# Side stages of a hybrid encoder layer, placed anew among its matmuls: later delta inverses, gates by themselves, scores two tiles ahead, x loaded earlier

## The chip, the cores and the metric

The kernel runs on one core of one Trainium2 chip. The metric is the device time of one execution in microseconds (us); where several runs are given, their median counts. The engines are named as the profile names them: PE is TensorE, DVE is VectorE, ACT is ScalarE, POOL is GpSimd, and SP is SyncE, whose instruction stream issues the DMAs.

## The reference, cut to what matters

One layer of an encoder works on 2048 prompt rows (zero state) and on 64 sample rows of a running stream (past of 2048 rows). A projection feeds four mixers with four heads of 64 each; their outputs are normed, gated and projected, and an MLP follows:

```python
proj = jnp.matmul(x, w_in)                       # 1024 -> 3856 columns, split among the mixers
o_a, gdn_s_new = _gated_delta(qa, ka, va, beta, g, gdn_s)     # A: chunks, triangular solve, state
o_b = _stick_breaking(qb, k_all, v_all, past)                 # B: attention with a running sum over keys
h_c, ... = _mlstm(qc, kc, vc, i_pre, log_f, c, n, m)          # C
o_d, ... = _hgrn2(silu(q), k_d, v, log_f, s)                  # D
mix = jnp.matmul(o, w_out);  x = layernorm(ALPHA * x + mix)
x = layernorm(ALPHA * x + jnp.square(relu(x @ w1 + b1)) @ w2 + b2)
```

In A each chunk needs the inverse of a unit lower triangular matrix (`triangular_solve(eye + lm, rhs)`), and a state that goes from chunk to chunk. In B the weight of a key is `exp(log_sigmoid(z) + after)`, where `after` sums over all later keys, so the key tiles of a query block depend on each other through a carry.

## The kernel before

The 2048 rows are 16 token tiles of 128, in four blocks of four tiles; block 0 also takes the sample's 64 rows. Two tiles make a unit, and the sample is a unit of its own: nine units. Every product with a large matrix is done with three matmuls on a split of both factors into a rounded part and a remainder (`mm3`, L463 to L466: `whi`/`wlo` of the weights, `XH`/`XL` of x, which `split_T`, L478 to L480, makes with transposes). A weight tile is read once into a ring `raw` (L455), split by ACT (L456) and POOL (L457), written to DRAM and read back from there whenever it is used again.

The program's stages are generators. `dense()` runs the projection of the four blocks and then the MLP of the four blocks, with the mixing of outputs (`mix`) in between; it is the main one. The others are `places()` (x into place, transposed), `delta()` (per unit: `gates`, then `gdn`), `memories()` (`mlstm`, `hgrn`) and `attend()`. `interleave` (L404) puts their pieces into one order by a clock of its own: a piece yields (PE time, delay until the next piece is due). The main stage goes first whenever it is due; the others get a turn when the main stage can't go, or when `EVERY` = 2.5 us of that clock have passed. `flag` and `need` order the stages among each other. Only PE keeps exactly this order. The order of DVE, ACT, POOL and SP is made by the framework's scheduler, which takes what its own estimate says is ready first; every engine then runs its list strictly in order.

Pieces of these stages that matter here:

- `gdn` (L870 on): per unit the conv, the products of keys and queries (L927, L928), transposes (L936, L937), then a solve of 16x16 blocks on DVE in 15 steps (L959 to L965) whose results go through DRAM (`ud`, `wd`) into the tiles `W` and `WT`. Two rounds of doubling follow for a unit of 128-row chunks: L994 multiplies the masked `cu` (POOL, L988) with `WT`, L1001 the result with `W`, L1009 transposes back; L1017 and L1024 do the last doubling. Then each chunk runs the recurrence (L1038 to L1059). The delay before the first L994 is 30 us of the planner's clock.
- `gates` (L762 to L838): small tiles, transposes, and row vectors through DRAM. It stands in `delta()` ahead of `gdn` of the same unit; its PSUM tiles come from the delta rule's ring (tag `m`, one bank) and its rows from the ring `g1`.
- `attention` (L1323 on), for each head: for each key tile `scores` (L1352, L1353), `stick` (the bound on DVE, L1317 or L1320; exp and ln on ACT, L1282 and L1283), `add_carry` (a row added on DVE, L1292; a cast on ACT, L1294; a remainder on POOL, L1295), `sums` (L1302, L1303: PE sums over later keys with a triangular matrix), `weights` (DVE L1309, ACT L1310 and L1312, DVE L1313) and `add_up` (L1362, L1363). Scores of the next key tile are issued right behind the `sums` of this one.
- `into_place` (L568): a tile of x is loaded in two halves from the ring `x2` (L486), one tile ahead of its transposes. `x2` also holds what leaves the projection.

## Time and profile before

| what | us |
|---|---|
| time, median of 3 runs | 3519.49 (3518.52 to 3526.22) |
| the profiled execution: its own time | 3528.34 |
| the profiled execution: its span | 3526.4 |
| PE busy in it | 3181.5 (90%) |
| DVE, ACT and POOL busy | 2239.1, 1345.4, 841.9 |
| mean granted clock of PE | 0.946 |

The span is that of the instructions in the trace; the execution's own time has about 2 us around it. PE's busy time counts a matmul from start to end although matmuls overlap, so it isn't PE at its peak. A row of PE's groups gives, behind the last bar, how long PE sat idle just before such an instruction, and what ended that.

### The profile page before, as it was taken

What the parts mean: (1) busy time and instruction counts of PE and PEld (TensorE: products, weight loads), DVE (VectorE), ACT (ScalarE), POOL (GpSimd) and SP (SyncE); (2) the same over time, 40 slices, a digit from 0 to 9 for tenths busy, and PEclk for the clock granted to TensorE, in tenths of its full rate; (3) what the DMA queues carried; (4) which work ended last, traced back from release to release, by engine and by line L of the source; (5) the groups of instructions that cost most, each with busy time, mean ns of one, the idle gap of its engine ahead of it and who ended that gap; (6) DMA issues with size and microseconds to landing.
All of it is one profiled execution on the core that took longest, in us unless ns stands there. A gap on an engine that the chain in (4) does not pass through costs nothing.

```text
span 3526.4 us, 60129 instructions
## 1 busy us (share of the span) xinstructions
PE 3181.5 (90%) x20906; PEld 2704.2 (77%) x20906; DVE 2239.1 (63%) x5360; ACT 1345.4 (38%) x3048; POOL 841.9 (24%) x946
## 2 busy tenths in 40 slices
PE   6897899898986988898898699999799999999998
PEld 6897888887875876676777488778577888888997
DVE  1566546344576777869688877787777554564445
ACT  2343433322343454654555454454454311121111
POOL 3342112101133134444435311221322100010001
PEclk8999998999998998999999799899899999999999
DMA  6986675566675875586678555567657587865552
GB/s 220 296 284 188 179 243 173 175 212 187 214 243 171 267 239 186 177 263 220 201 235 280 171 173 187 155 226 213 192 174 249 189 262 236 273 214 166 161 164 87
DMA packets 576268, 735.63 MB, mean 209 GB/s; under 512 B 104745, under 2 KB 301021, under 8 KB 575965
## 3 DMA queue, kind: packets, MB, share of 16 engines
q1 hardware_dynamic: 575964, 731.79, 64.9%
q8 instruction: 166, 2.72, 0.3%
q14 instruction: 138, 1.12, 0.1%
HBM read 548.63 MB, written 182.94 MB: 207 GB/s over the span
## 4 chain that ended last, share of the span: by engine, by line
PE 59%; DVE 17%; DMA 11%; SPq 4%; issue 4%; ACT 3%; POOL 2%; POOLq 0%; DVEq 0%; ACTq 0%
PE d L464 16%; PE d L465 16%; PE d L466 16%; DMA wlo<-wsp 1%; SPq L195 1%; DVE acc L1639 1%; DMA g<-qkv 1%; DMA vv<-x 1%; PE d L527 1%; PE a L1303 1%; DMA x<-in_x_prompt_dram 1%; DVE acc L1564 1%; DVE g L959 1%; POOL ar L1295 1%; DVE g L884 1%
## 5 line engine op out<-in xcount | busy, mean ns | idle before, releaser
L464 PE MATMUL d<-XH,whi 128*128 128x512 f32 (+1 forms) x1840 | 675.6, 367 | 3.7 <-ACT whi L456 3.0
L465 PE MATMUL d<-XL,whi 128*128 128x512 f32 (+1 forms) x1840 | 661.0, 359 | 1.0 <-DVE XL L480 0.9
L466 PE MATMUL d<-XH,wlo 128*128 128x512 f32 (+1 forms) x1840 | 659.8, 359 | 0.5 <-POOL wlo L457 0.5
L1639 DVE TENSOR_TENSOR acc<-d,acc 128x512 f32<-128x512 f32 x564 | 386.1, 687 | 177.6 <-PE d L466 164.7
L1295 POOL TENSOR_TENSOR ar<-as,ar 128x512 fp32r<-128x512 f32 (+3 forms) x177 | 198.2, 1120 | 956.5 <-ACT ar L1294 840.0
L464 PE MATMUL d<-whi,hh 128*128 128x512 f32 x992 | 404.9, 408 | 12.6 <-ACT x L1618 4.2
L465 PE MATMUL d<-wlo,hh 128*128 128x512 f32 x992 | 396.2, 399 | 0.1
L466 PE MATMUL d<-whi,hh 128*128 128x512 f32 x992 | 396.0, 399 | 0.0
L464 PEld LDWEIGHTS d<-XH,whi 128*128 128x128 f32 x1840 | 352.4, 192 | 53.7 <-ACT whi L456 3.2
L466 PEld LDWEIGHTS d<-XH,wlo 128*128 128x128 f32 x1840 | 351.7, 191 | 52.3 <-POOL wlo L457 0.9
L465 PEld LDWEIGHTS d<-XL,whi 128*128 128x128 f32 x1840 | 352.2, 191 | 46.6 <-DVE XL L480 1.4
L457 POOL TENSOR_TENSOR wlo<-raw,whi 128x512 fp32r<-128x512 f32 (+1 forms) x204 | 272.7, 1349 | 319.5 <-ACT whi L456 235.9
L464 PE MATMUL d<-whi,XH 128*128 128x256 f32 (+1 forms) x1024 | 316.3, 309 | 26.3 <-DMA whi<-wsp 15.4
L465 PE MATMUL d<-wlo,XH 128*128 128x256 f32 (+1 forms) x1024 | 307.9, 301 | 11.9 <-DMA wlo<-wsp 8.1
L466 PE MATMUL d<-whi,XL 128*128 128x256 f32 (+1 forms) x1024 | 305.3, 298 | 2.6 <-DVE XL L480 2.6
L1618 ACT ACTIVATE x<-d,cbig 128x512 f32<-128x512 f32 (+1 forms) x160 | 97.7, 610 | 506.4 <-PE d L466 502.6
L464 PEld LDWEIGHTS d<-whi,XH 128*128 128x128 f32 x1024 | 211.6, 207 | 32.5 <-DMA whi<-wsp 17.4
L464 PEld LDWEIGHTS d<-whi,hh 128*128 128x128 f32 x992 | 190.0, 192 | 57.2 <-ACT x L1618 5.1
L1620 DVE CAST hh<-x 128x512 fp32r<-128x512 f32 (+1 forms) x160 | 79.3, 496 | 236.2 <-ACT x L1619 235.8
L465 PEld LDWEIGHTS d<-wlo,XH 128*128 128x128 f32 x1024 | 211.3, 206 | 17.1 <-DMA wlo<-wsp 11.5
L466 PEld LDWEIGHTS d<-whi,hh 128*128 128x128 f32 x992 | 189.5, 191 | 44.4
L465 PEld LDWEIGHTS d<-wlo,hh 128*128 128x128 f32 x992 | 190.0, 192 | 41.2 <-DMA wlo<-wsp 0.8
(437 smaller groups left out, 6334.0 us busy)
## 6 DMA issues: line engine op xcount, KB each, us to landing
whi<-wsp SPq DMA_DIRECT2D x644, 256.0 KB
wlo<-wsp SPq DMA_DIRECT2D x644, 256.0 KB
wsp<-whi SPq DMA_DIRECT2D x196, 256.0 KB
wsp<-wlo SPq DMA_DIRECT2D x196, 256.0 KB
raw<-in_w_dram SPq DMA_DIRECT2D x128, 256.0 KB
raw<-in_w_in_dram SPq DMA_DIRECT2D x52, 256.0 KB
ak<-kk SPq DMA_DIRECT2D x80, 128.0 KB
ak<-vv SPq DMA_DIRECT2D x80, 128.0 KB
```

The source lines that it names most:

```text
L195: SP.dma_start(dst if dst.dtype == F32 else dst.bitcast(F32), src if src.dtype == F32 else src.bitcast(F32))
L457: POOL.tensor_tensor(lo, raw, hi.bitcast(F32), ALU.subtract)
L464: PE.matmul(out, lhsT=lh, rhs=rh, start=start, stop=False)
L465: PE.matmul(out, lhsT=lh, rhs=rl, start=False, stop=False)
L466: PE.matmul(out, lhsT=ll, rhs=rh, start=False, stop=stop)
L527: PE.matmul(pt, lhsT=lhs(k), rhs=r, start=k == ks[0] and i == 0, stop=k == ks[-1] and i == 1)
L884: DVE.scalar_tensor_tensor(dst[:, i], xin[:, i, j : j + N], convw(2 * p + i, j), dst[:, i], ALU.mult, ALU.add)
L959: DVE.tensor_tensor(tb[:PB, :m, :m], wb[:PB, i + 1 :, i + 1 :].rearrange("p j c -> p c j"), ub[:PB, i, i + 1 :].unsqueeze(1).to_broadcast( ...
L1295: POOL.tensor_tensor(sl, sp, sh.bitcast(F32), ALU.subtract)
L1618: ACT.activation(r, pt, AF.Relu, bias=b1c(ff))
L1620: DVE.tensor_copy(h[:, f, cs], r)
L1639: lambda pt, first, acc=acc: DVE.tensor_tensor(acc, pt, acc, ALU.add),
```

## The change

- The delays in `gdn` are raised: 30 to 50 before the first L994, 2.5 to 3.0, 2.0 to 3.5, 3.5 to 4.0, 3.0 to 4.0 and 1.5 to 2.5 at later places.
- `gates` becomes a stage of its own, `rows_of()`, that may run up to two units ahead. Its PSUM tiles move to the bank of `memories` (tag `h`), its rows to a ring `rw` of three.
- `interleave` gets a second list: `places` and `attend` are looked at whenever the planner comes round; `rows_of`, `delta` and `memories` still get a turn every 2.5 us. A channel-major step yields twice as often.
- `attention` issues the scores and `stick` of two key tiles at the start, and then those of tile x+2 behind the sums of tile x; the carry for tile x+1 is added directly behind the weights of tile x. Its delay goes from 7 to 6.5.
- `into_place` loads all tiles of a block at once, whole rows into the ring `acc`; `start` loads x1 at a flag `soon`, ahead of the free place.
- Rings: `raw` 4 to 3, `as` 4 to 5, `ak` 4 to 6.

```diff
-W_RAW, W_SP = 4, 6
+W_RAW, W_SP = 3, 6
-R_AS, R_AR, R_AQ, R_AK, R_OB = 4, 4, 3, 4, 1
+R_AS, R_AR, R_AQ, R_AK, R_OB = 5, 4, 3, 6, 1
+    rw = ring("rw", UNIT, 3)
...
-    def interleave(main, others):
+    def interleave(main, alike, others):
...
-            if not moved or clock[0] - last >= EVERY:
-                for g in sorted([g for g in alive if g is not main and due[id(g)] <= clock[0]], key=lambda g: due[id(g)]):
-                    moved = step(g) or moved
-                    last = clock[0]
+            turn = not moved or clock[0] - last >= EVERY
+            for g in sorted([g for g in alive if g in alike or turn and g in others], key=lambda g: due[id(g)]):
+                if due[id(g)] <= clock[0] and step(g):
+                    moved = True
+                    if g in others:
+                        last = clock[0]
...
-                if k % 4 == 3 and k < KD - 1:
-                    yield 12 * n * MM, 0
+                if k % 2 == 1 and k < KD - 1:
+                    yield 6 * n * MM, 0
...
     def into_place(b):
-        nxt = load_T(b.tiles[0], b.tiles[0].x)
+        ld = []
+        for t in b.tiles:
+            ld.append(bp.tile([P, 4 * UNIT], F32, tag="acc", name=nm("acc"), bufs=R_ACC)[:, :D])
+            SP.dma_start(ld[-1][: t.n], t.x)
+        if not b.i:
+            yield 0, 4
         for j, t in enumerate(b.tiles):
-            xt = nxt
             if b.i:
                 yield from need("xfree", b.i, j)
-            yield from put_T(t, t.off, xt)
-            if j + 1 < len(b.tiles):
-                nxt = load_T(b.tiles[j + 1], b.tiles[j + 1].x)
+            yield from put_T(t, t.off, [ld[j][:, 512 * g : 512 * g + 512] for g in range(2)])
...
-        pc = ps([C, 2 * w])
+        pc = ph([C, 2 * w])
...
-        ra, rb, rc = g1([68, N]), g1([68, N]), g1([68, N])
+        ra, rb, rc = rw([68, N]), rw([68, N]), rw([68, N])
...
-            yield (0.9, 30) if bs == 16 else (0.8, 2.5)
+            yield (0.9, 50) if bs == 16 else (0.8, 3.0)
...
-                yield 0.8 if j else 2.0, 2.0
+                yield 0.8 if j else 2.0, 3.5
...
-                z, carry, prev = scores(*its[0]), None, None
-                pe = 0.5
+                st, pe, prev = [], 0.5, None
+                for x in range(min(2, len(its))):
+                    z = scores(*its[x])
+                    st.append(stick(z, bound_diag if its[x][0].b is b else bound_plain))
+                    yield 0.5, 1
+                if its[2][0] not in kv:
+                    kv[its[2][0]] = fetch(its[2][0])
+                s2 = add_carry(st[0][1], None)
                 for x, (u, t) in enumerate(its):
-                    zc, sp = stick(z, bound_diag if u.b is b else bound_plain)
-                    sh, sl = add_carry(sp, carry)
-                    yield pe, 7
-                    carry = sums(sh, sl, lowk)
+                    yield pe, 6.5
+                    c = sums(*s2, lowk)
                     if prev:
                         add_up(*prev)
+                    if x + 2 < len(its):
+                        z = scores(*its[x + 2])
+                    if x + 3 < len(its) and its[x + 3][0] not in kv:
+                        kv[its[x + 3][0]] = fetch(its[x + 3][0])
+                    prev = (x, u, t, *weights(st[x][0], c))
                     if x + 1 < len(its):
-                        z = scores(*its[x + 1])
-                        if x + 2 < len(its) and its[x + 2][0] not in kv:
-                            kv[its[x + 2][0]] = fetch(its[x + 2][0])
-                    prev = (x, u, t, *weights(zc, carry))
-                    carry = carry[0:1, :]
+                        s2 = add_carry(st[x + 1][1], c[0:1, :])
+                    if x + 2 < len(its):
+                        st.append(stick(z, bound_diag if its[x + 2][0].b is b else bound_plain))
...
     def start(b):
+        yield from need("soon", b.i)
+        nxt = load_T(b.tiles[0], b.tiles[0].x1)
         yield from need("xfree", "m", b.i)
-        nxt = load_T(b.tiles[0], b.tiles[0].x1)
...
-    def delta():
+    def rows_of():
         for u in units:
...
+            if u.i >= 2:
+                yield from need("dl", u.i - 2)
+                yield from need("mh", u.i - 2)
             yield from need("gates", u.b.i)
             yield from gates(u)
             flag("rows", u.i, after=4.0)
+
+    def delta():
+        for u in units:
+            yield from need("rows", u.i)
             yield from need("qkv", u.b.i)
             yield from gdn(u)
...
-        interleave(dense(), [places(), delta(), memories(), attend()])
+        interleave(dense(), [places(), attend()], [rows_of(), delta(), memories()])
```

The changed file has other line numbers: L994 becomes L1000, `sums` L1308 and L1309, the bound L1323, the carry L1298, the weights L1315 and L1319, the load of x L577.

How the change moves instructions is shown at three places. The first is DVE, in the middle of a head's key tiles (`as` are the tiles of `stick`, `a` the PSUM tiles of scores and sums). Before, the weights of a tile come first (L1309), then the bound of the next (L1317), other work, and last the carry (L1292):

```order
L1309 TENSOR_TENSOR as_22892<-as_22892,a_23002 128x512
L1317 TENSOR_SCALAR as_23022<-a_23009 128x512
L940 TENSOR_TENSOR g_4701_23037<-m_23032,cbig 128x256
L941 TENSOR_TENSOR g_4702_23038<-m_23032,cbig 128x256
L1313 TENSOR_TENSOR ar_23019<-as_22892,ar_23018 128x512
L1292 TENSOR_TENSOR as_23023<-as_23023,a_23002 1x512
```

In the change the carry (L1298) stands directly behind the weights (L1315), and the bound (L1323) is for the tile after the next:

```order
L1315 TENSOR_TENSOR as_17851<-as_17851,a_18093 128x512
L1298 TENSOR_TENSOR as_18030<-as_18030,a_18093 1x512
L1323 TENSOR_SCALAR as_18116<-a_18098 128x512
L1653 TENSOR_TENSOR acc_17900<-d_18121,acc_17900 128x512
L1319 TENSOR_TENSOR ar_18108<-as_17851,ar_18107 128x512
```

So the carry no longer stands behind the bound, nor behind the exp and ln that follow the bound on ACT.

The second is PE, where the first L994 of the fourth unit stands (block 1's first; `m` is the delta rule's PSUM ring). Before, 142 rows stand between the unit's last L937 and this L994, 84 of them of the large products:

```order
L527 MATMUL d_13199<-wlo_13103,oh_12897 128x512
L527 MATMUL d_13199<-whi_13112,oh_12897 128x512
L527 MATMUL d_13199<-wlo_13113,oh_12897 128x512
L994 MATMUL m_13206<-g_2396_12728,g_2397_12737 64x64 x16
L1302 MATMUL a_13224<-ar_13091,XH 128x512
L1303 MATMUL a_13224<-ar_13092,XH 128x512
```

In the change 317 rows stand between, 288 of them of the large products:

```order
L468 MATMUL d_13162<-whi_13129,XH 128x264
L469 MATMUL d_13162<-wlo_13130,XH 128x264
L470 MATMUL d_13162<-whi_13129,XL 128x264
L1000 MATMUL m_13191<-g_2323_12424,g_2324_12433 64x64 x16
L1308 MATMUL a_13209<-ar_13107,XH 128x256
L1309 MATMUL a_13209<-ar_13108,XH 128x256
```

So the same product now has about twice the matmuls ahead of it since the transposes of its unit.

The third is SP at the program's start (`raw` are weights, `x` and `acc` tiles of x). Before:

```order
L486 DMA x_214_418<-in_x_prompt_dram 128x512
L455 DMA raw_380<-in_w_in_dram 128x2x256
L455 DMA raw_390<-in_w_in_dram 128x2x256
L365 DMA cbig<-in_gdn_A_log_dram 128x4
L486 DMA x_215_420<-in_x_prompt_dram 128x512
L455 DMA raw_400<-in_w_in_dram 128x2x256
L455 DMA raw_410<-in_w_in_dram 128x2x256
L486 DMA x_218_436<-in_x_prompt_dram 128x512
```

In the change whole tiles of x come one after the other, and the fourth weight tile isn't among them; it stands 12 rows further down, behind two more tiles of x, three stores of split weights and six small transfers:

```order
L577 DMA acc_418<-in_x_prompt_dram 128x1024
L459 DMA raw_380<-in_w_in_dram 128x2x256
L459 DMA raw_390<-in_w_in_dram 128x2x256
L366 DMA cbig<-in_gdn_A_log_dram 128x4
L577 DMA acc_420<-in_x_prompt_dram 128x1024
L459 DMA raw_400<-in_w_in_dram 128x2x256
L339 DMA g_6_159<-in_b_dram 32x128
L338 DMA g_6_159<-in_gdn_conv_w_dram 24x128
L340 DMA g_6_159<-in_out_norm_g_dram 8x128
L341 DMA g_6_159<-in_hgrn_lb_logits_dram 2x128
L577 DMA acc_422<-in_x_prompt_dram 128x1024
```

So block 0's x is asked for before the fourth weight tile instead of tile by tile between stores.

More of the change, by code (lines that the diff above doesn't have):

```diff
@@ L402, in need @@
             yield 0, done[key] - clock[0]
-    def interleave(main, others):
-        due = {id(g): 0.0 for g in [main] + others}
-        alive = [main] + others
+    def interleave(main, alike, others):
+        due = {id(g): 0.0 for g in [main] + alike + others}
+        alive = [main] + alike + others
         last = 0.0
@@ L505, in chan_mm @@
                 mm3(pt, h[:, k % 4, :], l[:, k % 4, :], *x_at(k, slice(o0, o0 + n)), k == 0, k == KD - 1)
-                if k % 4 == 3 and k < KD - 1:
-                    yield 12 * n * MM, 0
+                if k % 2 == 1 and k < KD - 1:
+                    yield 6 * n * MM, 0
             evac(o0, n, pt)
-            yield 12 * n * MM, 0
+            yield 6 * n * MM, 0
     def chan_major(b, w, c0, evac):
@@ L802, in gates @@
         A, B, Q = slice(0, 4), slice(32, 36), slice(64, 68)
-        ra, rb, rc = g1([68, N]), g1([68, N]), g1([68, N])
+        ra, rb, rc = rw([68, N]), rw([68, N]), rw([68, N])
         for z in (((1, ra[Q]), (2, rb[Q])), ((0, ra[A]), (3, ra[B]))):
             yield 0.3, 4
-            pr = ps([4, 2, N])
+            pr = ph([4, 2, N])
             for x, (k, dst) in enumerate(z):
@@ L832, in gates @@
         yield 0.3, 7
-        pm = ps([C, n, 4])
+        pm = ph([C, n, 4])
         for j in range(n):
@@ L1034, in gdn @@
             sl = slice(j * C, (j + 1) * C)
-            yield 1.0, 3.5
+            yield 1.0, 4.0
             pk = ps([C, 4, 64])
@@ L1041, in gdn @@
             DVE.tensor_tensor(R, R, c.vb, ALU.add)
-            yield 0.5, 3.0
+            yield 0.5, 4.0
             pv = ps([C, 4, 64])
@@ L1047, in gdn @@
             ACT.copy(vn, pv)
-            yield 0.5, 1.5
+            yield 0.5, 2.5
             po = ps([C, 4, 64])
@@ L1457, in attention_sample @@
             sh, sl = add_carry(sp, carry)
-            yield 0.5, 6
+            yield 0.5, 7
             c = sums(sh, sl, lows if j is None else lowk)
@@ L1588, in start @@
                 nxt = load_T(b.tiles[j + 1], b.tiles[j + 1].x1)
-            yield 0, 1.5 if j else 4
+            yield 0, 2
             yield from put_T(t, t.moff, xt)
@@ L1668, in mlp @@
                 ld = yield from mix_load(g)
+            if sb == ns - 1 and nxt:
+                flag("soon", nxt.i)
             yield from up(sb)
@@ L1718, in dense @@
             yield from project(b, dict(zip(MIX_0, mlps[0].groups)) if last else {})
+        flag("soon", 0)
         flag("xfree", "m", 0)
```

## The prediction

> **What bounds the kernel now.** The page's busy times come first, then the table of busy times by stretch (columns: stretch, its length, then PE, PEld, DVE, ACT and POOL busy with counts, PE's granted clock, DMA share, GB/s):
>
> ```profile
> PE 3181.5 (90%) x20906; PEld 2704.2 (77%) x20906; DVE 2239.1 (63%) x5360; ACT 1345.4 (38%) x3048; POOL 841.9 (24%) x946
> ```
>
> ```profile
> 0.00:85.00 85.00, 58.31 (x359) 54.87 (x360) 16.26 (x35) 20.39 (x45) 28.99 (x76) 0.86 0.71 224
> 85.00:1003.00 918.00, 831.86 (x6494) 758.67 (x6492) 471.25 (x1485) 318.87 (x811) 188.89 (x246) 0.94 0.70 216
> 1003.00:1536.00 533.00, 450.00 (x3199) 369.58 (x3198) 410.65 (x963) 261.69 (x606) 203.21 (x209) 0.91 0.65 213
> 1536.00:2162.00 626.00, 541.14 (x3446) 433.54 (x3445) 503.19 (x1121) 320.01 (x704) 234.23 (x232) 0.93 0.66 216
> 2162.00:2738.00 576.00, 531.48 (x3425) 428.26 (x3425) 435.63 (x1016) 273.70 (x599) 137.90 (x156) 0.95 0.64 201
> 2738.00:3526.00 788.00, 768.75 (x3994) 659.32 (x3992) 402.08 (x742) 150.73 (x285) 48.67 (x29) 0.99 0.60 195
> 762.00:2162.00 1400.00, 1213.56 (x8166) 1000.21 (x8165) 1030.44 (x2449) 659.48 (x1498) 468.39 (x486) 0.93 0.66 213
> 1320.00:2024.00 704.00, 593.62 (x3911) 472.32 (x3910) 575.24 (x1268) 363.64 (x808) 311.70 (x303) 0.92 0.66 217
> ```
>
> PE sets the time: it has the same matmuls in the same number after the change, so only its idle time, 3526.4 - 3181.5 = 345 us, and its clock can move. From 2738 us on, where only the MLP runs, there is little of either (19 us idle, clock 0.99). Before that idle time and a clock under 0.96 go together. The missing clock, (1 - clock) times length over the first six rows, is 195 us: 12 + 55 + 48 + 44 + 29 + 8. Third, PE's groups with the idle time in front of them and what ended it:
>
> ```profile
> L1302 PE MATMUL a<-ar,XH 128*128 128x512 f32 (+3 forms) x177 | 71.9, 406 | 41.3 <-ACT ar L1294 41.2
> L1303 PE MATMUL a<-ar,XH 128*128 128x512 f32 (+3 forms) x177 | 71.4, 404 | 29.6 <-POOL ar L1295 29.4
> L478 PE MATMUL d<-cbig,x 128*128 128x128 f32 (+1 forms) x272 | 48.6, 316 | 45.9 <-DMA x<-in_x_prompt_dram 29.9 <-DVE h L1201 5.8 <-DMA x<-x1d 5.2
> L994 PE MATMUL m<-g,g 64*64 64x64 f32 (+1 forms) x528 | 32.2, 272 | 73.6 <-DMA g<-wd 37.8 <-POOL g L988 35.6
> L1009 PE MATMUL m<-cbig,g 64*64 64x64 f32 (+2 forms) x132 | 17.8, 260 | 10.6 <-DVE g L1002 10.6
> L1045 PE MATMUL m<-g,g 128*128 128x64 f32 (+1 forms) x136 | 18.6, 284 | 6.8 <-DVE g L1041 6.8
> L1053 PE MATMUL m<-g,g 128*128 128x64 f32 (+1 forms) x136 | 17.8, 276 | 6.1 <-ACT g L1047 6.1
> ```
>
> The delta rule's first product (74 us), attention's sums (71), transposes of x (46) and three later delta steps (23.5) hold 214 of the 345 us. The change touches exactly these.
>
> **A, the delay before L994: -65 us.** The longest of these waits, and the price of a large matmul:
>
> ```profile
> 1033.65 0.42 PE L937 MATMUL m<-cbig,g 128*128 128x128 f32 x1
> 1086.38 0.44 PE L994 MATMUL m<-g,g 64*64 64x64 f32 x2 [17.30 <-DMA g<-wd]
> 1091.59 0.40 PE L464 MATMUL d<-whi,oh 128*128 128x512 f32 x1
> 1091.83 0.40 PE L465 MATMUL d<-wlo,oh 128*128 128x512 f32 x1
> ```
>
> From the end of L937 (1034.1) to L994 the chain (solve on DVE, blocks through DRAM) took 52 us. A 512-wide matmul follows the one before after 0.24 us, narrower ones in proportion. Counted so, the matmuls between L937 and L994 (front's second place) come to 27 us before and 50 now. Over all units with a wait the same count gives 25 to 30 us before and 46 to 52 now. PE takes some 10% longer than such a count, so the cover is 51 to 57 us, against chains of 36 to 58 us measured from the end of L937. Of 73.6 us, 0 to 16 stay; I take 8.5. An L994 that comes 23 us later holds nobody up: the product behind it in PE's list is another stage's.
>
> **B, attention: -45 us.** One key tile, with its wait:
>
> ```profile
> 1473.76 0.67 DVE L1309 TENSOR_TENSOR as<-as,a 128x512 f32<-128x512 f32 x1
> 1475.15 0.68 DVE L1317 TENSOR_SCALAR as<-a 128x512 f32<-128x512 f32 x1
> 1480.74 0.68 DVE L1292 TENSOR_TENSOR as<-as,a 1x512 f32<-1x512 f32 x1
> 1482.12 0.50 PE L1302 MATMUL a<-ar,XH 128*128 128x512 f32 x1 [1.69 <-ACT ar L1294]
> 1484.39 0.79 PE L1303 MATMUL a<-ar,XH 128*128 128x512 f32 x1 [1.77 <-POOL ar L1295]
> L1292 DVE TENSOR_TENSOR as<-as,a 1x512 f32<-1x512 f32 (+3 forms) x160 | 91.2, 570 | 33.2 <-ACT as L1283 29.2
> ```
>
> The carry (L1292) began 6.3 us after the weights (1474.4), since the bound, exp, ln and other work stood between. In the change it stands right behind the weights (front's first place). Measured in the same way for the 160 carries of the group below, that gap has a median of 3.0 us, and it is the part of the chain that goes. Against this the planner puts the sums closer: the matmuls between two sums come to a median of 9.5 us before and 8.1 now. The net is 1.6 us more slack for each tile; taken off the 35 waits that make up the 71 us, about 26 stay. The bounds are 20 us gained (if busy engines eat the slack) and 60.
>
> **C, x: -30 us.** Of 45.9 us nearly all wait for loads of x, in block 0 and at the turn to a new block:
>
> ```profile
> PE d L478 <- DMA x<-in_x_prompt_dram: 14.6, 5, 4.1
> 299.89 1.09 PE L478 MATMUL d<-cbig,x 128*128 128x128 f32 x4 [4.56 <-DMA x<-in_x_prompt_dram]
> ```
>
> (The first row is from the waits in 0 to 60 us.) The loads now come a block ahead, so behind block 0 they are done long before; the first load (some 4 us) and the wait for DVE (5.8) stay, and a few us of crowding. Bounds 20 to 38.
>
> **D, later delta steps: -12 us.** L1009, L1045 and L1053 wait 23.5 us; their delays rise by 0.5 to 1.5 us where single waits were 2 to 5. Half goes; bounds 0 and 20.
>
> **E, the clock: -57 us.** A to D take 152 of 345 idle us, 44%. Of the 195 us of missing clock I count a third as falling on idle time, where it costs nothing; 44% of the remaining 130 is 57. Bounds 20 and 90. [...]
>
> ```profile
> 528.00:616.00 88.00, 79.88 (x727) 72.60 (x726) 53.02 (x160) 26.82 (x75) 18.46 (x29) 0.88 0.58 177
> PE d L464 <- DMA whi<-wsp: 2.5, 2, 1.4
> ```
>
> **F, DVE is packed more tightly: +37 us.** With `gates` off the delta rule's path, the planner finishes the last unit's recurrence after 1884 us of counted matmuls instead of 2100, and attention's last sums near 2000 instead of 2290. The same side work thus falls on fewer matmuls. The matmuls that took 762 to 2162 us now have beside them, by the DVE rows that wait for them at their lines' means, about 1140 us of DVE work; it was 1030. Without a limit this stretch would lose 94 us of idle time (47 A, 31 B, 8 C, 8 D) and 33 of clock: 1273 us, in which DVE would be busy 90%. The most it has shown for long is 575/704 = 82%. I take 87% because waits that kept DVE idle go as well: 1140/0.87 = 1310, +37. Bounds 0 (90%) and +117 (82%, 1390 us).
>
> **G, the rings and the start: +8 us.** `raw` has three buffers. SP, which issues in order, already waits for such a buffer, and the first remainders are late since POOL builds constants:
>
> ```profile
> SPq L455 <- POOL wlo L457: 47.5, 60, 3.3
> 11.35 4.98 POOL L457 TENSOR_TENSOR wlo<-raw,whi 128x512 fp32r<-128x512 f32 x4
> ```
>
> The fourth weight load can't go out before 12.6 us (11.35 plus a quarter of 4.98) and everything behind it on SP waits too; it went out at once before. Later the loads of weights wait mostly for `whi` to come free, and one buffer fewer shifts them a few us. Bounds 0 and 20. Edits that I cost at nothing: the finer yields (same matmuls), `gates` in the bank of `memories` (both are short; if they collide, some us), `as` and `ak` (more room).
>
> **Sum.** The execution's own time is 3528.3. -65 -45 -30 -12 = -152; -57; +37; +8: 3364.3. The median of the runs lies 8.8 us under this execution, so the forecast is **3356 us**.
>
> **Rivals.**
> - *DVE becomes the bound at its old share.* At 82% the stretch takes 1390 us instead of 1310: 3436. For it: DVE's 82% over 704 us while PE also waited. Against: those waits idled DVE.
> - *The chains grow with their cover.* About half of L994's 74 us is a wait for POOL's masked blocks (L988), which stand in line behind POOL's other work. If fuller engines stretch the solve and these masks by 15 us, A gains 25 instead of 65 and the clock 15 less: 3411. For it: the chains reach from 36 to 58 us in the same code, and the long ones lie where DVE is full. The change then doesn't do what it says: later products still wait.
> [...]
> - *Slower: PE waits for a DVE that stays at the share of this stretch.* It was 1030/1400 = 73.6%. If every wait that goes comes back as another, because the in-order lists of DVE and ACT now hold more work ahead of each carry, 1140/0.736 = 1549 us: 3356 + 239 = 3595. It turns slower than before where the share is under 1140/(1310 + 163) = 77%.
> - *Better:* all covers hold and DVE reaches 90%: about 3300.
>
> **How the numbers follow.** A difference of 0.2%, 7 us, is about what a measurement of this kernel can tell from no change. Chances: forecast 0.41, DVE at its old share 0.21, chains that grow 0.14, clock for long waits 0.10, slower 0.09, better 0.05. The range takes in the first four with the bounds of the unknown costs, 3280 to 3480, and leaves out the slower case and part of the better. Faster: 0.41 + 0.21 + 0.14 + 0.10 + 0.05, less 0.03 for ends of the second that reach the old time, 0.88; same 0.03; slower 0.09.
>
> **What would show it.** A: idle time in front of the product at L1000 under 20 us. B: in front of the sums (L1308, L1309) 20 to 35 us. C: in front of the transposes of x 10 to 20 us. E: a clock of 0.95 or more between 85 and 2000 us. F: the longest dense stretch with DVE at 85 to 90%, and PE waiting for DVE and ACT in front of many lines instead of a few. Wrong I would be if L1000 still waited for blocks from DRAM, or if new waits of PE for evacuations (`acc`, `x`) made up for those that went.

## The result, and the profile after

The changed kernel takes **3468.41 us** (median of 4 runs, 3462.92 to 3476.45), the kernel before 3521.8 beside it (4 runs): a ratio of 0.9849, with a 95% interval of 0.9826 to 0.9873. It is faster by 53 us, where 3356 and so 165 were forecast. Sign and range held; the size did not, by 112 us. Two executions below were disturbed (one of no_attn, 5470 us at a granted clock of 0.79, and one of no_attn_no_planner, 3568 us at 0.82); they are left out of the ratios.

The busy times, the same six stretches as before, and a seventh that holds as much matmul work as 762 to 2162 us did before (same columns). Work is an estimate from the columns of the matmuls, at the spacing that the large products have in a row, 0.24 us for 512 columns (0.12 for 256, in the kernel before at 900 us): 1045 us before and 1035 now, where PE was busy 1214 and 1232. It isn't the same matmuls: 9023 now, 8166 before, and of the large products 3725 of 256 columns or more, 3992 before. Side products stand in their place.

```profile
PE 3160.0 (91%) x20906; PEld 2686.4 (77%) x20906; DVE 2275.2 (66%) x5360; ACT 1342.0 (39%) x3048; POOL 860.7 (25%) x946
...
0.00:85.00 85.00, 58.28 (x399) 54.90 (x400) 20.37 (x43) 24.29 (x54) 31.62 (x78) 0.94 0.76 233
85.00:1003.00 918.00, 813.91 (x6893) 741.93 (x6892) 570.67 (x1791) 368.18 (x966) 221.95 (x300) 0.94 0.69 211
1003.00:1536.00 533.00, 460.04 (x3369) 379.75 (x3370) 431.42 (x1030) 280.09 (x642) 204.57 (x209) 0.91 0.67 216
1536.00:2162.00 626.00, 544.86 (x3845) 436.14 (x3831) 544.43 (x1184) 363.98 (x815) 285.94 (x275) 0.92 0.67 212
2162.00:2738.00 576.00, 570.78 (x2677) 459.94 (x2676) 344.46 (x636) 183.04 (x337) 76.90 (x64) 0.99 0.69 229
2738.00:3466.00 728.00, 712.18 (x3754) 613.73 (x3752) 363.86 (x680) 122.41 (x235) 39.74 (x22) 0.99 0.59 195
761.00:2176.00 1415.00, 1231.95 (x9023) 1015.35 (x9022) 1160.75 (x2752) 761.90 (x1755) 547.81 (x562) 0.92 0.67 211
```

PE's idle time is 3466.7 - 3160.0 = 307 us, 38 less than before. The missing clock of the first six rows is 171 us (before 195). The seventh row is the core of it: the same amount of matmul work lasts 1415 us instead of 1400, with 130 us more of DVE's work beside it. What was gained lies behind it, where less side work is left: the fifth row has 5 us of idle time and a clock of 0.99, where it had 45 us and 0.95.

PE's groups, first those that the change aimed at, then those that are new (line numbers after the change):

```profile
L1308 PE MATMUL a<-ar,XH 128*128 128x512 f32 (+3 forms) x177 | 72.9, 412 | 13.7 <-ACT ar L1300 7.4 <-ACT h L1268 3.4 <-DVE acc L1653 2.9
L1309 PE MATMUL a<-ar,XH 128*128 128x512 f32 (+3 forms) x177 | 68.5, 387 | 17.7 <-POOL ar L1301 17.7
L482 PE MATMUL d<-cbig,x 128*128 128x128 f32 (+1 forms) x136 | 21.4, 288 | 0.1
L482 PE MATMUL d<-cbig,acc 128*128 128x128 f32 (+1 forms) x136 | 22.7, 300 | 7.4 <-POOL cbig L295 4.3 <-DMA acc<-in_x_prompt_dram 3.1
L1000 PE MATMUL m<-g,g 64*64 64x64 f32 (+1 forms) x528 | 22.8, 238 | 13.8 <-DMA g<-wd 11.8 <-ACT g L1017 1.3 <-issue 0.4
L1015 PE MATMUL m<-cbig,g 64*64 64x64 f32 (+2 forms) x132 | 17.3, 254 | 0.0
L1051 PE MATMUL m<-g,g 128*128 128x64 f32 (+1 forms) x136 | 18.2, 278 | 15.5 <-DVE g L1047 15.5
L1059 PE MATMUL m<-g,g 128*128 128x64 f32 (+1 forms) x136 | 17.6, 274 | 2.3 <-ACT g L1053 2.3
...
L1369 PE MATMUL po<-ar,ak 128*128 128x512 f32 (+3 forms) x208 | 74.8, 363 | 19.9 <-DVE ar L1319 19.9
L468 PE MATMUL d<-XH,whi 128*128 128x512 f32 (+1 forms) x1840 | 678.6, 369 | 19.4 <-ACT whi L460 8.5 <-DVE as L1323 6.7 <-DVE x L607 2.3
L1118 PE MATMUL h<-h,h 128*128 128x256 f32 (+1 forms) x68 | 19.2, 408 | 13.8 <-DMA h<-mlq 13.8
L1242 PE MATMUL h<-h,h 64*32 64x32 f32 x528 | 20.2, 204 | 10.5 <-DVE h L1219 10.5
L468 PE MATMUL a<-aq,ar 128*128 128x128 f32 (+1 forms) x34 | 10.0, 294 | 9.5 <-ACT ar L1459 9.5
L1403 PE MATMUL a<-cbig,as 128*128 128x128 f32 x64 | 10.3, 286 | 10.9 <-ACT h L1104 7.8 <-ACT as L1399 3.2
```

The first eight hold 71 us where the same products waited 214 before: 143 gone, 152 forecast. The last six hold 84 us; their products waited about 10 before. So the waits aimed at went nearly as forecast, but PE's idle time as a whole fell by 38 us only: most of the gain came back as other waits, many of them small, for DVE, ACT and DMA. The question of the experiments is what brought them.

### The profile page after: what moved, and what is told of

The parts are those of the page before. It is cut to its first block, busy times and chain, and to the rows that moved or that the text cites. A ratio compares the mean times of both kernels' runs of the same rounds, so it can differ in the third digit from the quotient of the medians.

```text
span 3466.7 us, 60038 instructions
## 1 busy us (share of the span) xinstructions
PE 3160.0 (91%) x20906; PEld 2686.4 (77%) x20906; DVE 2275.2 (66%) x5360; ACT 1342.0 (39%) x3048; POOL 860.7 (25%) x946
## 3 DMA queue, kind: packets, MB, share of 16 engines
q14 instruction: 136, 1.11, 0.1%
## 4 chain that ended last, share of the span: by engine, by line
PE 43%; DVE 10%; DMA 2%; issue 1%; ACT 1%; SPq 1%; POOL 1%; POOLq 0%; DVEq 0%; ACTq 0%
PE d L468 13%; PE d L469 12%; PE d L470 12%; DVE acc L1653 1%; DVE g L890 1%; PE d L531 1%; DVE ar L1319 1%; DVE as L1315 0%; DVE g L965 0%; PE po L1369 0%; DVE as L1298 0%; PE a L1309 0%; SPq L196 0%; PE a L1358 0%; PE a L1308 0%
## 5 line engine op out<-in xcount | busy, mean ns | idle before, releaser
L1301 POOL TENSOR_TENSOR ar<-as,ar 128x512 fp32r<-128x512 f32 (+3 forms) x177 | 210.0, 1186 | 753.5 <-ACT ar L1300 617.0
L461 POOL TENSOR_TENSOR wlo<-raw,whi 128x512 fp32r<-128x512 f32 (+1 forms) x204 | 276.2, 1365 | 299.4 <-ACT whi L460 199.7
L468 PE MATMUL d<-whi,XH 128*128 128x256 f32 (+1 forms) x1024 | 307.2, 300 | 15.9 <-DMA whi<-wsp 10.4
L470 PE MATMUL d<-whi,XL 128*128 128x256 f32 (+1 forms) x1024 | 297.9, 291 | 1.2 <-DVE XL L484 1.1
L1634 DVE CAST hh<-x 128x512 fp32r<-128x512 f32 (+1 forms) x160 | 75.3, 471 | 272.3 <-ACT x L1633 272.1
L469 PEld LDWEIGHTS d<-wlo,XH 128*128 128x128 f32 x1024 | 203.2, 198 | 23.8 <-DMA wlo<-wsp 14.7
L468 PEld LDWEIGHTS d<-whi,XH 128*128 128x128 f32 x1024 | 203.6, 199 | 22.5 <-DMA whi<-wsp 12.3
```

Source lines behind the costliest of these rows:

```text
L461: POOL.tensor_tensor(lo, raw, hi.bitcast(F32), ALU.subtract)
L468: PE.matmul(out, lhsT=lh, rhs=rh, start=start, stop=False)
L469: PE.matmul(out, lhsT=lh, rhs=rl, start=False, stop=False)
L470: PE.matmul(out, lhsT=ll, rhs=rh, start=False, stop=stop)
L1301: POOL.tensor_tensor(sl, sp, sh.bitcast(F32), ALU.subtract)
L1634: DVE.tensor_copy(h[:, f, cs], r)
```

## Experiments

Ratios are against the kernel before, run beside each; 0.01 is 35 us.

**Each part alone.** All four have three raw buffers; the last three add one part of the change as it stands in the diff, with `as` and `ak` at four.

```diff
-W_RAW, W_SP = 4, 6
+W_RAW, W_SP = 3, 6
# delta_alone also
-            yield (0.9, 30) if bs == 16 else (0.8, 2.5)
+            yield (0.9, 50) if bs == 16 else (0.8, 3.0)
...
# x_alone also: into_place, start and the flag "soon"
+            SP.dma_start(ld[-1][: t.n], t.x)
...
# attn_alone also: the loop of attention
+                    c = sums(*s2, lowk)
...
+                        s2 = add_carry(st[x + 1][1], c[0:1, :])
...
```

> The kernel before with three buffers for the raw weights instead of four; nothing else. The ring theory (term G is what ate the gain): 20 us or more slower than before. The packing theory (the gain was eaten by fuller engines, the ring costs little): within 8 us of before. It is also what the next three are compared with, since they have three buffers too.

Measured: 1.0001 (0.9983 to 1.0018). Three buffers cost nothing.

> The kernel before with the longer delays of the delta rule alone, three raw buffers; gates stay inside the delta rule, nothing is packed tighter by them. Packing theory: the wait in front of the first product falls from 74 to under 20 us and most of it is kept, 45 to 65 us faster than the kernel with three raw buffers alone. Displacement theory (a wait that goes comes back behind another in-order list, whatever the packing): the same wait falls, but only 15 to 30 us are kept.

Measured: 0.9933 (0.9910 to 0.9956), 24 us faster.

> The kernel before with x fetched a phase early alone, three raw buffers. Packing theory: the transposes of x wait 10 us instead of 46 and 25 to 35 us are kept. Displacement theory: 5 to 15 us are kept, and the loads of weights in block 0 wait more (the part up to 800 us no shorter).

Measured: 0.9886 (0.9858 to 0.9914), 40 us faster.

> The kernel before with attention's scores two key tiles ahead, the carry right behind the weights and the deeper delays of its sums, alone; three raw buffers, four buffers for the sums' rows. Packing theory: the sums wait 25 to 35 us instead of 71 and 30 to 45 us are kept. Displacement theory: the sums wait the same 25 to 35 us, but 10 to 20 us are kept.

Measured: 1.0057 (1.0041 to 1.0074), 20 us slower. PE's groups of the delta rule alone (three rows), then of attention alone:

```profile
L994 PE MATMUL m<-g,g 64*64 64x64 f32 (+1 forms) x528 | 18.8, 220 | 0.0
L1302 PE MATMUL a<-ar,XH 128*128 128x512 f32 (+3 forms) x177 | 74.7, 422 | 77.3 <-ACT ar L1294 72.7 <-DVE acc L1639 4.5
L1303 PE MATMUL a<-ar,XH 128*128 128x512 f32 (+3 forms) x177 | 74.0, 418 | 36.3 <-POOL ar L1295 34.9 <-POOL g L956 1.1
```

```profile
L1302 PE MATMUL a<-ar,XH 128*128 128x512 f32 (+3 forms) x177 | 69.1, 391 | 13.7 <-ACT ar L1294 12.3 <-ACT g L219 1.4
L1303 PE MATMUL a<-ar,XH 128*128 128x512 f32 (+3 forms) x177 | 66.9, 378 | 14.6 <-POOL ar L1295 14.6
L1363 PE MATMUL po<-ar,ak 128*128 128x512 f32 (+3 forms) x208 | 73.7, 358 | 14.0 <-DVE ar L1313 13.5 <-DVE cbig L228 0.5
L1136 PE MATMUL h<-h,h 128*128 128x130 f32 (+1 forms) x68 | 11.3, 290 | 11.2 <-POOL h L199 10.4 <-POOL h L1132 0.7
L464 PE MATMUL a<-aq,ar 128*128 128x128 f32 (+1 forms) x34 | 9.6, 282 | 10.4 <-DMA aq<-qh 10.4
L936 PE MATMUL m<-cbig,g 128*128 128x128 f32 (+1 forms) x34 | 9.2, 295 | 14.4 <-DVE acc L1646 7.9 <-DVE acc L1569 6.6
```

Both theories had a gain for attention alone; it lost. The delays empty L994 (69.8 us with three raw buffers, 0.0 here), and 22 us of it return at the sums (91 to 114): the displacement theory has this one. x keeps all of its gain. Attention's sums fall to 28 us, but four groups that waited 12 us together in the kernel before wait 50, and the kernel is slower. So no single theory covers the parts.

**DVE's work.** Four variants of the changed kernel, all with `ak` at four. The first has four raw buffers, and is otherwise the changed kernel.

```diff
# dve_more
-        DVE.tensor_scalar(zc, z, 0.125, LIM, ALU.mult, ALU.min)
+        for _ in range(2):
+            DVE.tensor_scalar(zc, z, 0.125, LIM, ALU.mult, ALU.min)
# hh_on_act, and dve_less
-                    DVE.tensor_copy(h[:, f, cs], r)
+                    ACT.copy(h[:, f, cs], r)
# dve_less alone
-        DVE.tensor_tensor(al, zc, ah.bitcast(F32), ALU.subtract)
+        POOL.tensor_tensor(al, zc, ah.bitcast(F32), ALU.subtract)
```

> The changed kernel with four buffers for the raw weights instead of three, and four for attention's keys instead of six. Ring theory (term G): the three raw buffers cost the part up to 600 us of PE's work some 20 us, so this is 15 us or more faster than the changed kernel. DVE theory: within 8 us of it (3460 to 3477). It is also the control for the next three, which have four key buffers.

Measured: 0.9894 (0.9879 to 0.9908), 16 us slower than the changed kernel by the ratios. A fourth raw buffer brings nothing here either; two key buffers fewer may cost this, though hh_on_act below, which has them too, does not show it. This control is uncertain by some 20 us.

> The changed kernel with attention's upper bound computed twice into the same tile: some 90 us more of DVE's work in all, 62 to 70 of it in the dense stretch (L1323 there: 62.2 us x103). The result is the same. DVE theory (the dense stretch lasts as long as its DVE work over 0.82): 75 to 85 us slower there, and the time 3540 to 3555. Order theory (DVE's share follows from waits in order, there is slack on it): 0 to 25 us slower, 3465 to 3495, with the DVE's share of the stretch up at 85% or more.

Measured: 0.9956 (0.9940 to 0.9973): 22 us slower than the control, 38 slower than the changed kernel, for 79 to 91 us more of DVE's busy time. Between both theories.

> The changed kernel with the MLP's rounded copy of h moved from DVE to ACT (L1634: 75 us in all, 20 of it in the dense stretch). DVE theory: 25 us faster there, 3435 to 3450. Order theory: within 10 us of the changed kernel, and PE waits more for ACT in front of the MLP's second product.

Measured: 0.9822 (0.9791 to 0.9853), 10 us under the changed kernel, 25 under the control. Against the control that is what the DVE theory had, against the changed kernel what the order theory had: it doesn't decide.

> The changed kernel with two DVE operations moved: that copy to ACT, and the remainder of attention's weights (L1319) from DVE to POOL. 108 us of DVE's work leave the dense stretch, of 1161. DVE theory: 80 to 130 us faster, 3340 to 3390. Order theory: between 30 us faster and 15 slower, the chain from the weights to the sums is one slower engine longer, and DVE's share of the stretch falls to 75 to 77% with the stretch as long as before.

Measured: 0.9897 (0.9876 to 0.9919), the same as the control. These kernels have PE's list in the same order, so here the stretch does hold the same matmuls: in the control, in dve_more, hh_on_act and dve_less:

```profile
771.00:2194.00 1423.00, 1233.66 (x9022) 1016.37 (x9022) 1151.76 (x2744) 759.92 (x1747) 549.39 (x561) 0.92 0.66 210
```

```profile
774.00:2226.00 1452.00, 1246.18 (x9024) 1026.73 (x9023) 1211.95 (x2849) 765.36 (x1749) 548.65 (x561) 0.91 0.65 205
```

```profile
767.00:2175.00 1408.00, 1227.55 (x9022) 1013.25 (x9021) 1133.62 (x2709) 779.65 (x1784) 545.36 (x561) 0.92 0.67 211
```

```profile
761.00:2188.00 1427.00, 1232.61 (x9025) 1017.18 (x9023) 1122.40 (x2595) 777.45 (x1782) 662.99 (x675) 0.92 0.65 208
```

DVE's share is 81%, 83%, 81% and 79%. It is no fixed bound: 60 us more work raise the share and lengthen the stretch by 29, half of that work. In hh_on_act 18 us less come with a stretch 15 us shorter, less than the control is uncertain by. In the last run DVE lost only 29 us there, not 108, since its other operations got longer (last section), and the stretch is no shorter; POOL and ACT got that work, so it is a weak test.

**Without attention's part.** The whole change but the loop of attention (no_attn), then also without gates as a stage (and with four raw buffers), then also without the planner's rules instead; and no_attn with a longer delay.

```diff
# no_attn: loop and rings of attention as before
-R_AS, R_AR, R_AQ, R_AK, R_OB = 5, 4, 3, 6, 1
+R_AS, R_AR, R_AQ, R_AK, R_OB = 4, 4, 3, 4, 1
# no_attn_no_gates also
-        interleave(dense(), [places(), attend()], [rows_of(), delta(), memories()])
+        interleave(dense(), [places(), attend()], [delta(), memories()])
# no_attn_no_planner instead (interleave and yields as before)
+        interleave(dense(), [places(), rows_of(), delta(), memories(), attend()])
# no_attn_wait8: no_attn, and
-                    yield pe, 7
+                    yield pe, 8
```

> The changed kernel without its part on attention (scores one key tile ahead, old delays and old rings of attention); everything else of the change stays. Attention theory (term B has the wrong sign: the deeper order brings back more waits than it takes): 15 to 30 us faster than the changed kernel, 3440 to 3455, the sums wait 60 us or more again, and PE's waits for DVE fall by 30 us or more. Packing theory (B is right, gates and the planner eat the gain): 20 to 45 us slower, 3490 to 3515.

Measured: 0.9943 (0.9924 to 0.9961), 33 us slower than the changed kernel (17 slower than after_raw4, which has four key buffers too). So in the whole attention's part, its loop with its rings, gains 33 us; my attention theory falls.

> The kernel before with the delta rule's delays, x a phase early and the new planner's rules; no change of attention, gates still inside the delta rule, four raw buffers, all rings as before. Attention theory: the two parts alone (0.9933 and 0.9886 of before) add up to 0.982, the planner adds nothing: 3450 to 3475. Packing theory: gates as a stage of their own cost 20 us or more by packing, so this is 20 us or more faster than the same kernel with them (the run with no change of attention).

Measured: 0.9870 (0.9842 to 0.9898), 26 us faster than no_attn: with the planner's rules, gates as a stage cost what the packing theory said. The fourth raw buffer is the only other difference, and three cost nothing above.

> The kernel before with the delta rule's delays, x a phase early and gates as a stage of their own; no change of attention, the planner's rules as before, three raw buffers. Attention theory: 3450 to 3475, as the sum of the two parts alone. Packing theory: within 15 us of the changed kernel or slower, since gates and the delta rule fill the stretch up to 1700 us of PE's work with 100 us more of DVE's work.

Measured: 0.9771 (0.9739 to 0.9803), and 0.9787 in a second run. By their mean, 0.9779, it is 25 us faster than the changed kernel, and 58 faster than no_attn, which has only the planner's rules more. That was the surprise: the planner's edit is dear; I had costed its finer yields at nothing and its list not at all.

> The changed kernel without its part on attention, and with the old delay of attention's sums raised from 7 to 8 us, so that the cover grows and the chain stays. Attention theory: the sums' waits fall by 20 to 35 us against the run without the part, and half of it or more is kept, 10 to 20 us faster than that run. Displacement theory: the sums' waits fall, the waits for DVE and ACT elsewhere rise as much, within 8 us of that run.

Measured: 0.9861 (0.9835 to 0.9886), 29 us faster than no_attn, more than either theory had.

**The planner's two halves.** The kernel without attention's part and without the planner's rules, again, with one half each, and with the longer delay.

```diff
# finer_yields
-                if k % 4 == 3 and k < KD - 1:
-                    yield 12 * n * MM, 0
+                if k % 2 == 1 and k < KD - 1:
+                    yield 6 * n * MM, 0
# own_list
-        interleave(dense(), [places(), rows_of(), delta(), memories(), attend()])
+        interleave(dense(), [places(), attend()], [rows_of(), delta(), memories()])
```

> The same kernel as the run with neither attention's part nor the planner's rules, once more, since its profiled execution was disturbed. It should repeat its 3447 within 8 us. Planner theory: its waits in front of the sums and of products that follow DVE and ACT are 60 us smaller in all than those of the kernel with the planner's rules (310 us idle), 230 to 260 us idle.

Measured: 0.9787 (0.9764 to 0.9811). The time repeats; PE's idle time is 286 us, more than the planner theory had.

> That kernel with one half of the planner's edit: the dense products offer their place to other stages after every second weight tile, not every fourth, so steps of 6 columns' time instead of 12. Yield theory (the finer places put side products nearer to what they wait for): 30 to 60 us slower than that kernel, 3480 to 3505. List theory (the other half does it): within 10 us of it, 3437 to 3457.

Measured: **0.9666 (0.9641 to 0.9691), 3404.82 us**, the fastest of all kernels here; the opposite of the yield theory, and outside the list theory's range too.

> That kernel with the other half of the planner's edit: attention and the places may take a step whenever they are due, the delta rule, its gates and the memories only every 2.5 us. List theory (attention no longer waits its turn, so the time between its weights and its sums is the bare delay of 7, where it was the delay and up to 2.5 us of waiting): the sums wait 50 us or more longer, 30 to 60 us slower, 3480 to 3505. Yield theory: within 10 us of it, 3437 to 3457.

Measured: 0.9881 (0.9850 to 0.9912), 36 us slower than without it (0.9779, the mean of two). The sums waited 40 us longer (first own_list, then no_planner_again):

```profile
L1308 PE MATMUL a<-ar,XH 128*128 128x512 f32 (+3 forms) x177 | 74.4, 420 | 78.1 <-ACT ar L1300 73.0 <-DVE h L1248 2.6 <-DVE cbig L226 2.4
L1309 PE MATMUL a<-ar,XH 128*128 128x512 f32 (+3 forms) x177 | 73.3, 414 | 44.9 <-POOL ar L1301 44.9
```

```profile
L1305 PE MATMUL a<-ar,XH 128*128 128x512 f32 (+3 forms) x177 | 71.3, 403 | 51.0 <-ACT ar L1297 46.7 <-DVE cbig L229 3.2 <-ACT g L1034 0.9
L1306 PE MATMUL a<-ar,XH 128*128 128x512 f32 (+3 forms) x177 | 70.6, 399 | 32.0 <-POOL ar L1298 32.0
```

> That kernel with the delay of attention's sums at 8 us instead of 7. List theory: the sums' wait under the old planner falls by some 20 us and 5 to 20 us are kept: 3427 to 3442, the best of all. Displacement theory: within 8 us of it.

Measured: 0.9847 (0.9819 to 0.9875), 24 us slower. A delay that pays where attention has a list of its own (no_attn_wait8) costs where it waits its turn already.

With finer yields on both sides the list alone is the difference between finer_yields and no_attn: 0.9666 to 0.9943, 98 us. Both from the start to some 2700 us, in three stretches that hold the same matmul work in both, and the sums of attention that fall in the middle one. First finer_yields:

```profile
0.00:724.00 724.00, 654.64 (x5446) 603.27 (x5447) 393.36 (x1238) 273.16 (x712) 189.77 (x287) 0.96 0.75 233
724.00:2078.00 1354.00, 1198.62 (x8490) 990.05 (x8489) 1064.96 (x2591) 679.52 (x1551) 491.03 (x511) 0.94 0.70 222
2078.00:2621.00 543.00, 518.38 (x2983) 416.64 (x2982) 390.83 (x791) 246.45 (x502) 118.58 (x120) 0.98 0.67 209
...
L1305 PE MATMUL a<-ar,XH 128*128 128x512 f32 (+3 forms) x93 | 38.7, 416 | 35.3 <-ACT ar L1297 31.8 <-ACT whi L457 2.1 <-DVE acc L1643 1.3
L1306 PE MATMUL a<-ar,XH 128*128 128x512 f32 (+3 forms) x93 | 38.9, 418 | 34.2 <-POOL ar L1298 34.2
```

And no_attn, which has the list:

```profile
0.00:747.00 747.00, 654.17 (x5506) 604.12 (x5507) 400.20 (x1334) 285.99 (x750) 200.11 (x296) 0.94 0.73 224
747.00:2202.00 1455.00, 1240.66 (x9012) 1011.76 (x9011) 1139.18 (x2744) 762.31 (x1743) 536.73 (x567) 0.92 0.65 205
2202.00:2708.00 506.00, 504.38 (x2404) 407.24 (x2403) 319.10 (x578) 170.41 (x310) 73.55 (x61) 1.00 0.70 231
...
L1308 PE MATMUL a<-ar,XH 128*128 128x512 f32 (+1 forms) x113 | 51.4, 455 | 43.0 <-ACT ar L1300 41.0 <-DVE XL L484 1.0 <-ACT x L1625 0.9
L1309 PE MATMUL a<-ar,XH 128*128 128x512 f32 (+1 forms) x113 | 50.8, 450 | 48.8 <-POOL ar L1301 48.5
```

In the middle stretch stand 93 key tiles without the list and 113 with it (94 before the change, 113 in the changed kernel), and 74 us more of DVE's work. It takes 101 us longer, and the next one gives back 37. Of the 101 us, 42 are PE's busy time (1198.62 to 1240.66: 522 more matmuls, and a clock of 0.92 instead of 0.94), and 59 its idle time (155 to 214). Of the idle time the sums have 22 us more (69.5 to 91.8), and one product, L1118, 23 more: it waits 31.3 us for `mlq` in no_attn and 8.0 in finer_yields.

The key tiles by themselves are not the price. no_attn_no_gates has the list, the finer yields and the same 113 key tiles in a stretch of the same matmul work, but its gates stand in the delta rule:

```profile
735.00:2141.00 1406.00, 1218.83 (x8115) 996.67 (x8114) 1078.87 (x2497) 713.72 (x1574) 490.06 (x500) 0.92 0.66 210
```

It is 49 us shorter than with gates as a stage, with 60 us less of DVE's work. The list brings attention forward; gates as a stage bring the delta rule and the memories forward (4328 instead of 3273 matmuls of theirs in the stretch, tags `m` and `h`). The stretch gets long where both come together.

**Is it DVE, and does attention's part need the list?** The bound twice in the kernel without planner and attention; and the kernel before with the delays, attention's part and finer yields.

> The kernel with neither attention's part nor the planner's rules (3447 and 3451 in two runs), with attention's upper bound computed twice, as in the run of the changed kernel that had it. The result is the same. Packing theory (DVE is near its limit only where the list packs the side work): 60 us more of DVE's work cost little here, 0 to 15 us, 3450 to 3465, where they cost the packed kernel 24 to 46. Rival (every microsecond of DVE costs half of itself anywhere): 25 to 45 us, 3475 to 3495.

Measured: 0.9879 (0.9849 to 0.9909): 35 us slower, for 72 us more of DVE's busy time: half of that work here too, by the whole run. The stretch without the second bound (no_planner_again) and with it:

```profile
733.00:2114.00 1381.00, 1207.45 (x8488) 996.25 (x8488) 1058.53 (x2590) 679.34 (x1551) 486.71 (x511) 0.93 0.68 217
```

```profile
731.00:2152.00 1421.00, 1224.60 (x8493) 1007.46 (x8492) 1094.57 (x2675) 687.23 (x1551) 485.56 (x511) 0.91 0.66 212
```

DVE's share is 77% in both, and 36 us more of its work come with 40 us. So DVE is not a limit that only the packed stretch meets, and its price is not the same everywhere.

> The kernel before with the delta rule's delays, attention's part and the finer places in the dense products; no list of its own for attention, no gates as a stage, x as before, three raw buffers. If attention's part costs 23 us wherever attention waits its turn (as it did alone): 3525 less 25 and 45, plus 23, 3470 to 3490. If it gains its 36 us here as well: 3410 to 3435.

Measured: 0.9931 (0.9908 to 0.9954), slower than both ranges. The delta rule's delays alone are as fast (0.9933). Finer yields gained 40 us in a kernel with x early and gates as a stage; what they are worth in this one without attention's part was not run, so that attention's part takes their gain back is likely, not shown.

Nor is it shown that attention's part needs the list. Where it lost time it had four `as` buffers, where it gained it had five. ACT's exp of `stick`, in attention alone and in the changed kernel:

```profile
L1282 ACT ACTIVATE as<-as 128x512 f32<-128x512 f32 (+3 forms) x177 | 97.5, 551 | 180.6 <-DVE ar L1313 93.9 <-DVE as L1317 39.6 <-DVE as L1320 28.9
```

```profile
L1288 ACT ACTIVATE as<-as 128x512 f32<-128x512 f32 (+3 forms) x177 | 97.5, 551 | 75.7 <-DVE as L1323 44.0 <-DVE as L1326 22.6 <-POOL ar L1301 4.2
```

With four buffers the exp waits 93.9 us for L1313 (106.0 in delta_attn_yields), the last operation that reads an earlier tile's `as` buffer; with five that wait is gone. Either the list or the fifth buffer may be what makes attention's part pay, and no run has one without the other.

The whole change with the list alone taken out, and attention's part with x but without the list, were not tried either.

## Why the prediction was right or wrong

- **A, B, C, D, the waits.** A to C are right in what they do: L1000 waits 13.8 us (forecast under 20), the sums 31 (20 to 35), the transposes of x 7.5 (10 to 20). So the rival with chains that grow, which left 49 us at L1000, doesn't hold. The three delta steps still wait 17.8 of their 23.5 us; half was to go. Wrong is that the terms add up: alone the delays are worth 24 us, not 65, and the sums took up 22 us of the wait that went; x is worth 40, not 30; attention's part gains 33 in the whole and loses 20 alone.
- **E, the clock.** 24 us of missing clock came back, not 57, and the sign that I gave, 0.95 or more between 85 and 2000 us, did not come (0.94, 0.91, 0.92). Idle time fell by 38 of 345 us, not by 152; by E's own rule that is 14 us of clock. No run shows the rule that gave the 57 (a third of the missing clock on idle time, the rest in proportion to idle time); the runs show 24 us of clock beside 38 of idle time. In the stretch of F none came back: 0.07 of 1400 us were missing before, 0.08 of 1415 after, and the idle time there stayed too. In E's rows the clock was 0.88 over 88 us in which PE's longest wait was 1.4 us; whether the clock follows all waits or only long ones, no run here tells.
- **F is the step that failed.** It read: "I take 87% because waits that kept DVE idle go as well: 1140/0.87 = 1310". Measured are 1161 us of DVE's work in 1415, 82.0%; the work is 21 us over its estimate, the stretch 105 of the missing 112 us. The waits did not go: PE's idle time in this stretch is 183 us, where it was 186 (1400 less 1213.56). The 1310 us stood for 1181 of PE's busy time (1213.56 less 33 of clock) and 129 idle (186 less 94 plus 37); measured are 1232 and 183. So 54 of the 105 us are idle time that stayed, 33 are E's clock, which stayed with it, and 18 are busy time that no term had. My rival with DVE at its old share, 1390 us for the stretch and 3436, had the size nearly right, but a fixed share is not what the runs show: it went from 77% to 83% among the kernels, and more work on DVE made a kernel slower at 77% as well as at 81%.
- **The cause I gave for the packing was the gates; it takes the list as well.** DVE's work in the stretch is 1030 us before, 1059 to 1065 with gates as a stage and the old planner, 1079 with the list and finer yields but no such gates, and 1139 with both (no_attn). The prediction has no term for the list, and it costed finer yields at nothing. Measured by one edit each, with gates as a stage and attention as before: the list costs 36 us, and 98 with finer yields; finer yields gain 40 without the list and lose 22 with it (0.9881 to 0.9943). With both of these, gates as a stage cost 26. List and attention's part together cost 64 us against finer_yields (0.9666 to 0.9849).
- **G.** Three raw buffers cost nothing (1.0001), not 8 us. The first stretch gained nothing in the whole (762 us before, 761 after). It has 736 with x alone, 735 in no_attn_no_gates and 747 in no_attn: what x gave, gates with the list and then attention's part took.
- **The slower rival** gave 1549 us for the stretch at DVE's share of 73.6%. The share rose to 82, above its break-even of 77.

What stays open: why PE idles more, and not less, where the side work is packed. At half of itself, DVE's work would explain 37 of the 101 us that the list costs in its stretch; in the loose kernel the same kind of work cost its full length. Chance has a part as well. The 23 us at L1118 come from where the planner happened to put one product, and a delay that is 1 us longer gained 29 us in no_attn and lost 24 without the planner's rules. So a difference of some 25 us from one placement does not show a mechanism by itself.

## What to carry to other kernels

A wait that was taken off PE was not gained in full here: with three raw buffers the delays took the wait at L994 to 0.0 us (69.8 without them), but PE's idle time fell by 37 us only (348.8 to 311.5). So a part of a change is to be timed alone and in company, with the same buffers in both: attention's part was worth minus 20 us or plus 33, and a list of the planner and a buffer lie between the two. Rules that let side stages run ahead are to be timed one by one and together: with finer yields, the list and gates as a stage together (0.9943) were slower than either without the other (0.9870 and 0.9666).

## What the hardware showed unexpectedly

Some of DVE's operations on tiles in SBUF took longer while POOL worked. In the run with less on DVE, two views of the same 2 us, DVE's timeline and POOL's (start, duration):

```profile
1403.86 1.38 DVE L1638 TENSOR_TENSOR hh<-x,hh 128x512 fp32r<-128x512 f32 x1 [1.92 <-ACT hh L1634]
1405.27 0.69 DVE L1315 TENSOR_TENSOR as<-as,a 128x512 f32<-128x512 f32 x1
...
1403.39 1.30 POOL L461 TENSOR_TENSOR wlo<-raw,whi 128x512 fp32r<-128x512 f32 x1
```

L1638 has both inputs in SBUF and took 1.38 us; L1315 behind it, with one input from PSUM, took 0.69 (its mean in that run is 0.68), with POOL at work beside it too (the next L461 began at 1405.18 and took 1.30). In the changed kernel 70 of the 96 L1638 of this shape had no POOL instruction beside them, with a median and a maximum of 0.69 us; 20 had one beside them for over half of their time, with a median of 1.11 (0.67 to 2.79). Over the whole run with less on DVE, L1204, all in SBUF, took 522 ns on average, against 412 in the control:

```profile
L1204 DVE TENSOR_TENSOR h<-h 128x128 f32<-128x128 f32 x96 | 50.1, 522 | 0.0
```

```profile
L1204 DVE TENSOR_TENSOR h<-h 128x128 f32<-128x128 f32 x96 | 39.5, 412 | 0.0
```

L1315 at 512 columns took 680 against 679. The moves took 75 us (L1634, to ACT) and 125 (L1319, to POOL) off DVE, but of the 85 costliest groups of DVE in each run, the 77 that both have took 63 us more in all. How much of these 63 us fell beside POOL's work was not counted.
